# First FFN of a decoder step: gate and up by Strassen's scheme, and the down product as a stage of its own

## The chip, the cores and the metric

The kernel runs on one core of a Trainium2 chip. The metric is the device time of one launch in microseconds. Three runs of the kernel before took 2860.6, 2861.0 and 2862.41 us; the median, 2861.0, is the time before.

## What is computed

One layer of a hybrid decoder in f32 over 1088 tokens: 1024 of a prompt and 64 of a sample group. D_MODEL is 1024 and D_FF 2816 (22 blocks of 128 hidden columns). Cut to what matters here:

```
def swiglu(x, w_gu, w_down):
    gate, up = jnp.split(x @ w_gu, 2, axis=-1)
    return (jax.nn.silu(gate) * up) @ w_down

x = x + 0.5 * swiglu(rmsnorm(x, ffn1_norm), ffn1_w_gu, ffn1_w_down)   # the first FFN: what changes
h = rmsnorm(x, mix_norm); z = h @ w_in                                # 58 column blocks: attention, recurrence,
                                                                      # memory, gates
x = x + merged @ w_out
x = x + 0.5 * swiglu(rmsnorm(x, ffn2_norm), ffn2_w_gu, ffn2_w_down)   # the second FFN
```

## The kernel before

Features lie on the 128 partitions and tokens along the free dimension. The 1088 tokens are three chunks of 352, 368 and 368 columns (`CH`). Every f32 operand is split into two float32r parts, a high part (ScalarE copies it) and the remainder (VectorE subtracts), and every product is three matmuls: high by high, high by remainder, remainder by high (`mac3`, L179 to L181). Weights come as [128, 1024] units: SyncE's queue loads one (`load`, L141), ScalarE and VectorE split it (`split`, L153 and L154) into one of four buffers, and `ahead` keeps them ahead of use.

The first FFN (`ffn`) goes over 22 pairs: a pair is one gate and one up tile of 128 hidden columns. For each pair and chunk there are two products of 8 k-tiles by 3 matmuls. The norm's scale per token is applied after the product, from the row tile `rbc`, when the pair is evacuated (`evac`: VectorE from PSUM, Silu on ScalarE, the product of the two on GpSimd, then the split into `h`). So the first matmul needs x, its gains and a weight, but no norm. `DOWN` interleaves the down product: after each two or three pairs their rows of w_down are used at once, `h` stays in SBUF, and each down tile is added into x by VectorE (L348).

Each engine works through its own queue in order, and the order is that of the code: `tick`, called inside the products, runs side jobs one step at a time (`first`, `side`, `due`). SyncE's queue alone is ordered by the framework's scheduler. Along the first FFN go copies of the sample caches (`copies`, from DRAM to DRAM, about 1 MB each) and three calls of `bias_rows`, each a small DMA and two matmuls (L399) that TensorE waits for in its queue. After the last down group `part` splits x for the next layer.

Of the kernel before, what the change touches and what calls it, by code (L numbers as in the profile page):

```python
# [15 lines left out]
D = 1024  # L16
# [23 lines left out]
# rows of w_down taken together, and the width of their column blocks; the last rows stay whole  # L40
DOWN = [(0, 2, 512), (2, 2, 512)] + [(k, 3, 256) for k in range(4, 19, 3)] + [(19, 3, 1024)]
# [9 lines left out]
class Kernel:  # L51
    def __init__(self, ctx, tc, ins, cst, outs):
        self.ctx, self.tc, self.nc = ctx, tc, tc.nc
        self.i, self.c, self.o = ins, cst, dict(zip(_OUTS, outs))
        self.n = 0
        self.ticks = 0
        self.first, self.side, self.due, self.hurry = [], [], [], False
        self.raws, self.ready, self.using = [], [], 0
# [39 lines left out]
    def bank(self, tag, name=None):  # L98
        w = 1024 if tag == "s" else 512
        return self.ps.tile([128, w], F32, name=self.uid(name or tag), tag=tag, bufs=self.ps_bufs[tag])  # L100

# [1 line left out]
    def make_plan(self):  # L103
# [6 lines left out]
        def ffn(gu, dn):  # L110
            pair = lambda p: [col(gu, p), col(gu, KF + p)]
            plan, off = pair(0) + pair(1), 0
            for g, (k, nk, w) in enumerate(DOWN):
                if w == D:
                    return plan + [flat(dn, off + j * 128 * D, D) for j in range(nk)]
                k1, n1, _ = DOWN[g + 1]
                plan += pair(k1) + [flat(dn, off + j * 128 * nk * w, nk * w) for j in range(D // w)]
                plan += [u for p in range(k1 + 1, k1 + n1) for u in pair(p)]
                off += 128 * nk * D

# [12 lines left out]
        self.plan = ffn("w_gu1", "w_dn1") + mix + merge + outp + ffn("w_gu2", "w_dn2")  # L133
# [10 lines left out]
    def split(self, cuts=1):  # L144
        nc = self.nc
        if not self.raws:
            self.load()
        if self.raws:
            name, raw, n = self.raws.pop(0)
            spl = self.wspl.tile([128, 2, 1024], F32R, name=self.uid("ws"), tag="wspl")  # L150
            for j in range(cuts):
                e = slice(j * n // cuts, (j + 1) * n // cuts)
                nc.scalar.activation(spl[:, 0, e], raw[:, e], AF.Copy)  # L153
                nc.vector.tensor_tensor(out=spl[:, 1, e], in0=raw[:, e], in1=spl[:, 0, e].bitcast(F32), op=OP.subtract)  # L154
            self.ready.append((name, spl))
        while len(self.raws) < 2 and self.plan:
            self.load()

    def ahead(self):
        if len(self.ready) + self.using < 4:  # L160
            self.split()

    def unit(self, name, w):
        """The next unit: (j, c) -> both parts of the 128 columns from c of its k-tile j, w columns wide."""
        if not self.ready:
            self.split()
        got, spl = self.ready.pop(0)
        assert got == name, (got, name)
        self.using += 1
        return lambda j, c, n=128: tuple(spl[:, s, j * w + c:j * w + c + n] for s in range(2))  # L170

    def done(self):
        self.using -= 1

    def mac3(self, out, wx):
        nc = self.nc
        n = len(wx)
        for i, ((wh, wl), (xh, xl)) in enumerate(wx):
            nc.tensor.matmul(out, wh, xh, start=i == 0, stop=False)  # L179
            nc.tensor.matmul(out, wh, xl, start=False, stop=False)  # L180
            nc.tensor.matmul(out, wl, xh, start=False, stop=i == n - 1)  # L181
# [19 lines left out]
    # ---- rstd of tokens from the feature-major sums of their squares: token-major first, then as rows on every  # L201
    # partition ----
# [28 lines left out]
    def sumsq(self, k, src, acc, n, eng=None, tag="td"):  # L231
        """Add the squares of one feature tile into acc."""
# [11 lines left out]
    def setup(self):  # L244
# [4 lines left out]
        self.wraw = pool("wraw", 3)  # L249
        self.wspl = pool("wspl", 4)  # L250
        self.xgp = pool("xgp", 3)
# [18 lines left out]
        self.xs_d = [self.dram([128, KD, n], f"xs_d{c}") for c, (_, n) in enumerate(CH)]  # L270
        self.gate_d = self.dram([24, 128, NT], "gate_d")
# [6 lines left out]
    def load_x(self):  # L278
        """The first chunk and weight in small pieces, one after the other."""
        nc = self.nc  # L280
        part = lambda c, k, n: nc.sync.dma_start(self.x[:, k:k + n, CH[c][0]:sum(CH[c])],
                                                 self.i["x"][k:k + n, :, CH[c][0]:sum(CH[c])].rearrange("k p n -> p k n"))
        part(0, 0, 2)
        self.load(2)
        for k in (2, 4, 6):
            part(0, k, 2)
        self.load()
        for c in (1, 2):
            for k in (0, 4):
                part(c, k, 4)  # L290
        nc.sync.dma_start(self.ident, self.c["ident"])

    def start_x(self, c):
        t0, n = CH[c]
        self.new_xg(c)
        for k in range(KD):
            if c == 0 and k == 2:
                self.split(2)
            self.split_x(c, k, self.x[:, k, t0:t0 + n], self.v["ffn1_norm"])
        if c == 0:  # L300
            self.split()

# [1 line left out]
    def ffn(self, gu, dn, order, begin, after, fill):  # L304
# [38 lines left out]
        def down_tile(ks, part, o, c):  # L343
            t0, n = CH[c]
            ps = self.mm_bank("pd")
            self.mac3(ps[:, :n], [(part(j), tuple(h[k][:, s, t0:t0 + n] for s in range(2))) for j, k in enumerate(ks)])
            xa = self.x[:, o, t0:t0 + n]
            nc.vector.tensor_tensor(out=xa, in0=xa, in1=ps[:, :n], op=OP.add)  # L348
            self.tick()

        gate_up(0)
        gate_up(1)
        for g, (k, nk, w) in enumerate(DOWN[:-1]):
            k1, n1, _ = DOWN[g + 1]
            gate_up(k1)
            for o0 in range(0, KD, w // 128):
                wd = self.unit(dn, w)
                for o in range(o0, o0 + w // 128):
                    for c in range(3):
                        down_tile(range(k, k + nk), lambda j: wd(j, (o - o0) * 128), o, c)  # L360
# [3 lines left out]
        k, nk, w = DOWN[-1]  # L364
        wd = [self.unit(dn, w) for _ in range(nk)]
        for c in range(3):
            for o in range(KD):
                down_tile(range(k, k + nk), lambda j: wd[j](0, o * 128), o, c)
# [37 lines left out]
    def toeplitz(self, dst, g, h, col, rows, n):  # L406
        """dst[r, j] = bias row [g, h] at col - r + j."""
# [30 lines left out]
    def heads(self, g, hp):  # L438
        """q, k and v of one pair of heads; the rest of their work is queued."""
# [40 lines left out]
    def att_job(self):  # L480
        """Prompt attention, three blocks at a time at different stages."""
# [66 lines left out]
    def att_combine(self, pool):  # L548
        """Mix the three head groups of the prompt tokens, 128 at a time."""
# [24 lines left out]
    def mix_groups(self, o, A, H):  # L574
        """o [128, 3, A, H*64 + H + H]: values, -max, sum per head of group g; the mix replaces the values of group 0."""
# [35 lines left out]
    def sample_take(self, g, hp, z):  # L611
        """Keep the sample columns of one pair of heads: token-major, and queries apart by head."""
# [38 lines left out]
    def sample_piece(self, src, g, b, u):  # L651
        """[128, n, 256]: rows dil*i + 4u + c of batch b of a cache of group g."""
# [6 lines left out]
    def sample_scores(self, g):  # L659
        """Scores of one group over the caches, [cache row, batch, head, token]."""  # L660
# [126 lines left out]
    def mem_prep(self, mp):  # L787
        """The memory tokens, scaled by the norm's gains and split, and their rstd."""
# [55 lines left out]
    def mem_head(self, h, pool):  # L844
        """One memory head's queries; returns its attention over the prompt as a job."""
# [699 lines left out]
```

## Time and profile before

| | |
|---|---|
| median of three runs | 2861.0 us |
| span of the profiled execution | 2854.3 us |
| what lies around the span, by the median | 6.7 us |
| TensorE matmul, busy | 2801.9 us, 98% of the span, 16762 matmuls |
| VectorE, ScalarE, GpSimd busy | 1309.6, 748.5, 449.0 us |
| HBM read and written | 268.0 and 84.2 MB |

The profile has one execution with the span from its first to its last instruction; no time of that execution from outside is given, so the 6.7 us are the median less the span. A matmul's recorded duration overlaps the next one, so the pace of TensorE is read from the distance between starts (the step), not from the duration. "Idle before" is the engine's idle time just ahead of an instruction, with what ended it.

### The profile page before, as it was taken

How to read it: one execution, taken by the hardware profiler on the slowest of the kernel's cores; microseconds unless marked ns; L12 is line 12 of the kernel's file. 1: busy time of each engine (PE TensorE's matmuls, PEld its weight loads, DVE VectorE, ACT ScalarE, POOL GpSimd, SP SyncE). 2: the span in 40 equal slices, each digit the busy share in tenths (PEclk: the TensorE clock that was granted, in tenths of full speed). 3: DMA queues.
4: the chain of work that ended last, by engine and by line, in shares of the span. 5: the costliest groups of instructions: out<-in, count | busy, mean ns of one | idle time of the engine just before them, and what ended most of it. 6: DMA issues, size and time to landing. Idle time of an engine off the chain costs nothing. (4 is left out here: it accounts for less than half of the span.)

```text
span 2854.3 us, 40939 instructions
## 1 busy us (share of the span) xinstructions
PE 2801.9 (98%) x16762; PEld 2685.4 (94%) x16762; DVE 1309.6 (46%) x2204; ACT 748.5 (26%) x1306; POOL 449.0 (16%) x504
## 2 busy tenths in 40 slices
PE   8999999999999999999989999899999999999998
PEld 7999999999999879999978888899999999999998
DVE  6433333333364433666685445664444333333244
ACT  4112111111253212233334334333321111111112
POOL 3001000000030000112143111332210000000104
PEclk9999999999999999999999999999999999999999
DMA  4222221221243342665544321765222122122121
GB/s 155 78 96 72 84 76 62 84 77 62 77 167 120 97 128 71 186 194 183 169 154 147 120 79 56 255 189 191 89 74 74 67 78 78 67 78 78 67 74 63
DMA packets 142107, 308.03 MB, mean 108 GB/s; under 512 B 17800, under 2 KB 95816, under 8 KB 141248
## 3 DMA queue, kind: packets, MB, share of 16 engines
q1 hardware_dynamic: 141920, 305.42, 32.6%
q8 instruction: 132, 2.16, 0.3%
q14 instruction: 55, 0.45, 0.0%
HBM read 267.97 MB, written 84.19 MB: 123 GB/s over the span
## 5 line engine op out<-in xcount | busy, mean ns | idle before, releaser
L179 PE MATMUL pg<-xg,ws 128*128 128x368 f32 (+1 forms) x2112 | 696.4, 330 | 6.1 <-ACT ws L153 6.1
L181 PE MATMUL pg<-xg,ws 128*128 128x368 f32 (+1 forms) x2112 | 694.4, 329 | 2.0 <-DVE ws L154 2.0
L180 PE MATMUL pg<-xg,ws 128*128 128x368 f32 (+1 forms) x2112 | 690.2, 327 | 0.5 <-DVE xg L199 0.5
L179 PE MATMUL z<-xg,ws 128*128 128x368 f32 (+1 forms) x1392 | 479.4, 344 | 6.0 <-DVE ta L1092 6.0
L181 PE MATMUL z<-xg,ws 128*128 128x368 f32 (+1 forms) x1392 | 457.0, 328 | 0.0
L180 PE MATMUL z<-xg,ws 128*128 128x368 f32 (+1 forms) x1392 | 456.1, 328 | 0.0
L154 DVE TENSOR_TENSOR ws<-wr,ws 128x1024 fp32r<-128x1024 f32 (+2 forms) x257 | 306.8, 1195 | 235.4 <-ACT ws L153 235.2
L179 PEld LDWEIGHTS pg<-xg,ws 128*128 128x128 f32 x2112 | 398.8, 189 | 6.4 <-ACT ws L153 6.1
L181 PEld LDWEIGHTS pg<-xg,ws 128*128 128x128 f32 x2112 | 398.9, 189 | 2.7 <-DVE ws L154 2.7
L180 PEld LDWEIGHTS pg<-xg,ws 128*128 128x128 f32 x2112 | 398.7, 189 | 2.4 <-DVE xg L199 2.4
L153 ACT ACTIVATE ws<-wr 128x1024 fp32r<-128x1024 f32 (+2 forms) x257 | 253.6, 989 | 543.6 <-PE pd L181 373.7
L180 PE MATMUL pd<-h,ws 128*128 128x368 f32 (+1 forms) x1056 | 346.2, 328 | 0.0
L179 PE MATMUL pd<-h,ws 128*128 128x368 f32 (+1 forms) x1056 | 346.0, 328 | 0.0
L181 PE MATMUL pd<-h,ws 128*128 128x368 f32 (+1 forms) x1056 | 345.5, 327 | 0.0
L321 POOL TENSOR_TENSOR td<-sl,tb 128x352 f32<-128x352 f32 (+1 forms) x132 | 128.4, 973 | 1336.7 <-DVE tb L320 1302.9
L179 PEld LDWEIGHTS z<-xg,ws 128*128 128x128 f32 x1392 | 263.2, 189 | 28.2 <-issue 19.0
L348 DVE TENSOR_TENSOR x<-x,pd 128x368 f32<-128x368 f32 (+1 forms) x384 | 199.0, 530 | 189.6 <-PE pd L181 189.5
L180 PEld LDWEIGHTS z<-xg,ws 128*128 128x128 f32 x1392 | 263.4, 189 | 2.8 <-issue 0.3
L181 PEld LDWEIGHTS z<-xg,ws 128*128 128x128 f32 x1392 | 262.8, 189 | 0.0
L320 DVE SCALAR_TENSOR_TENSOR tb<-pg,rbc 128x352 f32<-128x352 f32 (+1 forms) x132 | 70.7, 535 | 316.9 <-PE pg L181 316.9
L179 PEld LDWEIGHTS pd<-h,ws 128*128 128x128 f32 x1056 | 198.3, 188 | 0.0
L181 PEld LDWEIGHTS pd<-h,ws 128*128 128x128 f32 x1056 | 198.3, 188 | 0.0
(267 smaller groups left out, 3145.0 us busy)
## 6 DMA issues: line engine op xcount, KB each, us to landing
wr<-in_w_gu_dram SPq DMA_DIRECT2D x87, 512.0 KB
wr<-in_w_in_dram SPq DMA_DIRECT2D x58, 512.0 KB
qb<-qs_d SPq DMA_DIRECT2D x48, 512.0 KB
out_sk_dram<-in_cache_k_dram SPq DMA_DIRECT2D x16, 1020.0 KB
out_sv_dram<-in_cache_v_dram SPq DMA_DIRECT2D x16, 1020.0 KB
wr<-in_w_dn_dram SPq DMA_DIRECT2D x40, 384.0 KB
kv<-in_cache_k_dram SPq DMA_DIRECT2D x24, 512.0 KB
kv<-in_cache_v_dram SPq DMA_DIRECT2D x24, 512.0 KB
```

The source lines that it names most:

```text
L153: nc.scalar.activation(spl[:, 0, e], raw[:, e], AF.Copy)
L154: nc.vector.tensor_tensor(out=spl[:, 1, e], in0=raw[:, e], in1=spl[:, 0, e].bitcast(F32), op=OP.subtract)
L179: nc.tensor.matmul(out, wh, xh, start=i == 0, stop=False)
L180: nc.tensor.matmul(out, wh, xl, start=False, stop=False)
L181: nc.tensor.matmul(out, wl, xh, start=False, stop=i == n - 1)
L320: nc.vector.scalar_tensor_tensor(tb, pu[:, :n], 0.5, self.rbc[:, t0:t0 + n], op0=OP.mult, op1=OP.mult)
L321: nc.gpsimd.tensor_tensor(out=td, in0=sl, in1=tb, op=OP.mult)
L348: nc.vector.tensor_tensor(out=xa, in0=xa, in1=ps[:, :n], op=OP.add)
```

## The change

The tokens are two halves of 544, each a pair of chunks of 272. For a pair of tiles (gate, up), for the k-tiles 0 to 3 and 4 to 7 and for the two chunks of a half, the product is a 2 by 2 block product. It is now done with seven products of 4 k-tiles on sums of blocks (Winograd's form) in place of eight. The sums of weight blocks are made per pair (`combined`: seven operands of 512 columns, each split by ScalarE and VectorE; two sums on VectorE, two on GpSimd). The sums of x blocks are made once per half (`operands`), from x that has been scaled by gain and norm beforehand (`square_half`, `scale`). So the norm of a half comes ahead of its first matmul. Products come in the order m1, m6, m7, m5, m2, m4, m3 (`OPS`). m2, m4 and m3 accumulate into the banks of m1, m7 and m5 after ScalarE or VectorE has read these (`swiglu`).

A call of `quad` is one pair's seven products for one half or both. `QUADS` runs pairs 0 to 3 for the first half alone, during which the second half's operands are made; then pairs 4 to 21 for both; then pairs 0 to 3 for the second half. The result of each goes to DRAM (`h_d`). The down product follows as its own stage (`down`) in 11 groups of two blocks; `hidden` reads a block back and splits it. x itself is loaded again when the last four quads begin. Weights are split in halves of 512 columns into seven buffers, and raw weights have four buffers, in the whole kernel. The second FFN keeps its scheme.

```diff
-        self.wraw = pool("wraw", 3)
-        self.wspl = pool("wspl", 4)
+        self.wraw = pool("wraw", 4)
+        self.wspl = pool("wspl", RING)
...
+TC, TH = 272, 544
+OPS = (1, 6, 7, 5, 2, 4, 3)
+ALONE = 4
+QUADS = ([(p, (0,)) for p in range(ALONE)] + [(p, (0, 1)) for p in range(ALONE, KF)] + [(p, (1,)) for p in range(ALONE)])
+RING = 7
...
+    def combined(self, name, g, u):
+        a11, a12, a21, a22 = g[:, :512], g[:, 512:], u[:, :512], u[:, 512:]
...
+        put(1, a11)
+        yield
+        put(4, a22)
+        tt(nc.vector, a22, a21, a22, OP.add)
+        tt(nc.vector, s2, a22, a11, OP.subtract)
+        tt(nc.gpsimd, a21, a11, a21, OP.subtract)
+        yield
+        put(6, s2)
+        yield
+        put(7, a21)
...
+        put(2, a12)
+        tt(nc.gpsimd, a12, a12, s2, OP.subtract)
+        yield
+        put(3, a12)
...
+    def operands(self, tp, xs, g, pool, eng):
...
+        def put(m, src):
+            t = (pool[1] if m in (4, 3) else pool[0]).tile([128, 2, 4, TC], F32R, name=f"xo{tp}{m}{self.uid('_')}", bufs=1)
+            nc.scalar.activation(t[:, 0], src, AF.Copy)
+            nc.vector.tensor_tensor(out=t[:, 1], in0=src, in1=t[:, 0].bitcast(F32), op=OP.subtract)
...
+        def less(out, x, y):
+            eng.tensor_tensor(out=out, in0=x, in1=y, op=OP.subtract)
...
+    def swiglu(self, p, tp, pool):
...
+            if m == 7:
+                new("uu", [2, TC], 3)
+                plus(t["uu"][:, 1], ps, t["mu"])
...
+                nc.gpsimd.tensor_tensor(out=sl, in0=sl, in1=t["uu"], op=OP.mult)
+                nc.sync.dma_start(self.h_d[p, :, tp * TH:(tp + 1) * TH], sl.rearrange("p j n -> p (j n)"))
...
+    def hidden(self, k, pool):
+        raw = pool.tile([128, NT], F32, name=self.uid("hr"), tag="hr", bufs=2)
+        nc.sync.dma_start(raw, self.h_d[k])
+        yield
+        h = pool.tile([128, 2, NT], F32R, name=self.uid("h"), tag="h", bufs=4)
+        nc.scalar.activation(h[:, 0, :], raw, AF.Copy, scale=0.5)
+        nc.vector.scalar_tensor_tensor(h[:, 1, :], raw, 0.5, h[:, 0, :].bitcast(F32), op0=OP.mult, op1=OP.subtract)
...
+    def second():
+        yield from K.square_half(1, xs[1], ev)
+        yield from K.operands(1, xs[1], K.v["ffn1_norm"], (xo1, xo1b), nc.gpsimd)
+    K.first.append(second())
+    K.hurry = True
+    for n, (p, tps) in enumerate(QUADS):
...
+        if n == KF:
...
+            for c, (t0, w) in enumerate(CH):
+                nc.sync.dma_start(K.x[:, :, t0:t0 + w], K.i["x"][:, :, t0:t0 + w].rearrange("k p n -> p k n"))
+            for k, nk, _ in DOWN1[:2]:
+                K.first += [K.hidden(k + j, pool) for j in range(nk)]
+        K.quad("w_gu1", p, tps, ev)
```

Where this moves instructions is shown at two places. The first is VectorE's queue at the start of the program. Before, `xg` is the x operand of a chunk, `ws` a split weight; the rows up to the first two weights are:

```order
L199 SCALAR_TENSOR_TENSOR xg_116<-x_101,vec,xg_116 128x352 x2
L154 TENSOR_TENSOR ws_121<-wr_103,ws_121 128x512 x2
L199 SCALAR_TENSOR_TENSOR xg_116<-x_101,vec,xg_116 128x352 x6
L154 TENSOR_TENSOR ws_140<-wr_109,ws_140 128x1024
L199 SCALAR_TENSOR_TENSOR xg_168<-x_101,vec,xg_168 128x368 x8
```

Two k-tiles of x and half a weight are enough for the first matmul there. Now, at the same place on VectorE (`xs` is a half of x, `xo` an x operand, `rbc` the norm as rows), from the norm's rows to the operand of m6, the second product:

```order
L318 COPY rbc<-t_164 128x272
L179 TENSOR_TENSOR ws_170<-wr_111,ws_170 128x512
L383 SCALAR_TENSOR_TENSOR xs_105<-xs_105,vec,rbc 128x544 x4
L389 TENSOR_TENSOR xo_21_181<-xs_105,xo_21_181 128x1088
L393 TENSOR_TENSOR xs_105<-xs_105 128x4x272
L383 SCALAR_TENSOR_TENSOR xs_105<-xs_105,vec,rbc 128x544 x2
L179 TENSOR_TENSOR ws_187<-wr_113,ws_187 128x512
L194 TENSOR_TENSOR wr_113<-wr_113 128x512
L194 TENSOR_TENSOR s_169<-wr_113,wr_111 128x512
L383 SCALAR_TENSOR_TENSOR xs_105<-xs_105,vec,rbc 128x544 x2
L393 TENSOR_TENSOR xs_105<-xs_105 128x4x272
L389 TENSOR_TENSOR xo_23_196<-xs_105,xo_23_196 128x1088
```

The work that came after the products (the norm) now stands ahead of them, and scalings, block sums and seven operands of 1088 columns stand in front of what the later products wait for. The second place is SyncE's queue where the last four quads begin. Before, around the first FFN's last pairs, there are weights and a cache copy alone:

```order
L141 DMA wr_5843<-in_w_gu_dram 128x1024
L141 DMA wr_5914<-in_w_gu_dram 128x1024
L141 DMA wr_5985<-in_w_dn_dram 128x1024
L1259 DMA out_sk_dram<-in_cache_k_dram 16x16320
L141 DMA wr_6061<-in_w_dn_dram 128x1024
```

Now, with `sl` the results of the quad before, `x` the reload and `hr` a hidden block read back:

```order
L488 DMA h_d<-sl_5044 128x544
L488 DMA h_d<-sl_5058 128x544
L1486 DMA out_sk_dram<-in_cache_k_dram 16x16320
L1552 DMA x_5131<-in_x_dram 128x8x352
L1552 DMA x_5131<-in_x_dram 128x8x368 x2
L495 DMA hr_5151<-h_d 128x1088
L165 DMA wr_5172<-in_w_gu_dram 128x1024
```

The first hidden block stands behind the whole of x. VectorE's queue in the first of these quads is, from the add of m6 (`mu`) to the adds of m7 and m5 (`uu`):

```order
L465 TENSOR_TENSOR mu_5153<-pg_5155,mu_5153 128x272
L179 TENSOR_TENSOR ws_5190<-wr_4945,ws_5190 128x512
L194 TENSOR_TENSOR wr_4945<-wr_4945 128x512
L194 TENSOR_TENSOR s_5168<-wr_4945,wr_4943 128x512
L499 SCALAR_TENSOR_TENSOR h_5196<-hr_5151,h_5196 128x1088
L465 TENSOR_TENSOR uu_5199<-pg_5177,mu_5153 128x272
L179 TENSOR_TENSOR ws_5214<-s_5168,ws_5214 128x512
L465 TENSOR_TENSOR uu_5199<-pg_5201,uu_5199 128x272
```

The remainder of that hidden block stands ahead of the add of m7, and m4 accumulates into m7's bank.

## Rows read from the trace of the kernel before

**Rows 1.** The page: TensorE's busy time, and the chain by engine.
```profile
PE 2801.9 (98%) x16762; PEld 2685.4 (94%) x16762; DVE 1309.6 (46%) x2204; ACT 748.5 (26%) x1306; POOL 449.0 (16%) x504
...
PE 46%; DVE 1%; ACT 0%; DMA 0%; POOL 0%; issue 0%; SPq 0%; DVEq 0%; POOLq 0%; ACTq 0%
```
**Rows 2.** Stretches: length, busy time of the engines (instructions), granted clock, DMA share, GB/s.
```profile
0.00:100.00 100.00, 88.67 (x506) 85.49 (x507) 59.04 (x97) 41.34 (x72) 29.10 (x31) 0.98 0.37 127
100.00:816.00 716.00, 712.43 (x4306) 709.24 (x4306) 273.38 (x458) 142.48 (x225) 85.29 (x106) 1.00 0.24 80
816.00:2854.00 2038.00, 2000.84 (x11954) 1890.63 (x11952) 977.17 (x1651) 564.72 (x1010) 334.65 (x368) 0.99 0.36 117
```
**Rows 3.** Timeline of TensorE (start, duration): the first matmul, and the first FFN's end.
```profile
6.08 0.66 PE L179 MATMUL pg<-xg,ws 128*128 128x352 f32 x1 [6.08 <-ACT ws L153]
...
815.91 0.32 PE L179 MATMUL z<-xg,ws 128*128 128x352 f32 x1
```
**Rows 4.** Timeline of TensorE: products' first matmuls, 24 apart; then two, 30 apart.
```profile
414.10 0.33 PE L179 MATMUL pg<-xg,ws 128*128 128x352 f32 x1
...
417.98 0.33 PE L179 MATMUL pg<-xg,ws 128*128 128x368 f32 x1
...
421.98 0.33 PE L179 MATMUL pg<-xg,ws 128*128 128x368 f32 x1
...
853.15 0.28 PE L179 MATMUL mk<-mg,ws 128*128 128x256 f32 x1
...
856.71 0.28 PE L179 MATMUL mk<-mg,ws 128*128 128x256 f32 x1
```
**Rows 5.** TensorE's groups by shape up to 816 us; each has two more lines alike.
```profile
L179 PE MATMUL pg<-xg,ws 128*128 128x368 f32 x704 | 233.4, 332 | 0.0
...
L179 PE MATMUL pd<-h,ws 128*128 128x368 f32 x352 | 116.8, 332 | 0.0
L179 PE MATMUL pg<-xg,ws 128*128 128x352 f32 x352 | 116.4, 331 | 6.1 <-ACT ws L153 6.1
...
L179 PE MATMUL pd<-h,ws 128*128 128x352 f32 x176 | 56.6, 322 | 0.0
```
**Rows 6.** DMA in the first 24 us, in 40 slices of 0.6 us.
```profile
GB/s 0 0 8 113 113 334 408 385 325 295 364 359 380 399 432 406 380 407 390 366 353 356 363 393 397 395 400 405 407 410 423 416 430 416 408 254 35 0 0 0
```
**Rows 7.** VectorE's groups by shape up to 816 us: busy, mean ns.
```profile
L154 DVE TENSOR_TENSOR ws<-wr,ws 128x1024 fp32r<-128x1024 f32 x51 | 63.1, 1239 | 43.9 <-ACT ws L153 43.9
L348 DVE TENSOR_TENSOR x<-x,pd 128x352 f32<-128x352 f32 x64 | 33.0, 517 | 19.7 <-PE pd L181 19.7
...
L154 DVE TENSOR_TENSOR ws<-wr,ws 128x768 fp32r<-128x768 f32 x20 | 19.2, 959 | 22.4 <-ACT ws L153 22.4
```
**Rows 8.** ScalarE's split of a weight, whole program.
```profile
L153 ACT ACTIVATE ws<-wr 128x1024 fp32r<-128x1024 f32 x183 | 192.4, 1052 | 481.9 <-PE pd L181 373.7 <-PE pg L181 54.3 <-PE z L181 34.4
```
**Rows 9.** GpSimd's groups by shape, whole program.
```profile
L690 POOL TENSOR_TENSOR qb<-qb,kv 128x1024 f32<-128x1024 f32 x24 | 57.6, 2398 | 235.1 <-DMA qb<-qs_d 151.9 <-DVE s L510 23.8 <-DVE st L538 16.6
L216 POOL TENSOR_TENSOR rs<-rs,mhalf 128x4 f32<-128x4 f32 x13 | 15.1, 1162 | 59.7 <-DVE rs L215 32.1 <-DVE rs L213 17.5 <-DVE rs L207 10.0
```
**Rows 10.** Timelines: VectorE with GpSimd busy beside it, GpSimd there, VectorE alone.
```profile
9.10 6.65 DVE L199 SCALAR_TENSOR_TENSOR xg<-x,vec,xg 128x352 fp32r<-128x352 f32 x6
...
11.06 1.10 POOL L1291 TENSOR_TENSOR acc<-acc,td 128x352 f32<-128x352 f32 x1
...
20.82 7.44 DVE L199 SCALAR_TENSOR_TENSOR xg<-x,vec,xg 128x368 fp32r<-128x368 f32 x13
```
**Rows 11.** Timeline of TensorE at a call of `bias_rows`.
```profile
150.72 1.13 PE L399 MATMUL t<-oh 32*4 32x512 f32 x4 [3.56 <-DMA oh<-in_rel_bias_dram]
...
152.50 0.49 PE L179 MATMUL pg<-xg,ws 128*128 128x352 f32 x1
152.79 0.49 PE L180 MATMUL pg<-xg,ws 128*128 128x352 f32 x1
```
**Rows 12.** The first FFN's last 26 us as a stretch, columns as in rows 2.
```profile
790.00:816.00 26.00, 26.00 (x163) 25.93 (x162) 22.41 (x41) 16.52 (x34) 18.91 (x17) 1.00 0.32 116
```

More of the change, by code (lines that the diff above doesn't have):

```diff
@@ L142, in load, with raw @@
             self.raws.append((name, raw, n))
-    def split(self, cuts=1):
-        nc = self.nc
+    def raw(self):
         if not self.raws:
             self.load()
[L148 to L157, printed above, removed]
@@ L159, in ahead, with part @@
-    def ahead(self):
-        if len(self.ready) + self.using < 4:
-            self.split()
-    def unit(self, name, w):
[L165 to L170, printed above, removed]
+        return self.raws.pop(0)
+    def part(self, src):
+        nc = self.nc
+        n = src.shape[1]
+        spl = self.wspl.tile([128, 2, 512], F32R, name=self.uid("ws"), tag="wspl")
+        nc.scalar.activation(spl[:, 0, :n], src, AF.Copy)
+        nc.vector.tensor_tensor(out=spl[:, 1, :n], in0=src, in1=spl[:, 0, :n].bitcast(F32), op=OP.subtract)
+        return spl
@@ new lines, in make @@
+    def make(self):
+        for _ in self.rest:
+            return
+        if self.raws or self.plan:
+            name, raw, n = self.raw()
+            if name in self.strassen:
+                self.rest = self.combined(name, raw, self.raw()[1])
+            else:
+                self.rest = self.halves(name, raw, n)
+            next(self.rest)
+            while len(self.raws) < 2 and self.plan:
+                self.load()
+    def ahead(self):
+        for _ in range(2):
+            if len(self.ready) + self.using < RING:
+                self.make()
@@ L293, in start_x @@
-    def start_x(self, c):
-        t0, n = CH[c]
[L295 to L301, printed above, removed]
+        rb = self.rbc[:, tp * TH:(tp + 1) * TH]
+        block = lambda i, j: xs[:, 4 * i:4 * i + 4, j * TC:(j + 1) * TC]
+        b11, b12, b21, b22 = (block(i, j) for i in range(2) for j in range(2))
+        got = self.xo[tp] = {}
@@ new lines, in operands, with square_half @@
+        less(b21, b21, b22)
+        yield
+        put(4, b21)
+        yield
+    def square_half(self, tp, xs, pool):
+        nc = self.nc
+        acc = None
+        for k in range(KD):
+            t = pool.tile([128, TH], F32, name=self.uid("sq"), tag="sl" if k else "uu", bufs=3)
+            nc.scalar.activation(t, xs[:, k, :], AF.Square)
+            if k:
+                nc.vector.tensor_tensor(out=acc, in0=acc, in1=t, op=OP.add)
+            else:
+                acc = t
+            if k % 2:
+                yield
+        r = [self.rstd(TC, acc[:, j * TC:(j + 1) * TC]) for j in range(2)]
+        yield
+        for j in range(2):
+            self.rows(self.rbc[:, tp * TH + j * TC:tp * TH + (j + 1) * TC], r[j], TC)
+        yield
@@ new lines, in quad @@
+    def quad(self, gu, p, tps, pool):
+        banks, steps = {}, {tp: self.swiglu(p, tp, pool) for tp in tps}
+        for m in OPS:
+            w = self.operand(gu, m)
+            for tp in tps:
+                bank = {2: 1, 4: 7, 3: 5}.get(m, m)
+                if bank == m:
+                    banks[tp, m] = self.mm_bank("pg")
+                ps, xo = banks[tp, bank][:, :TC], self.xo[tp][m]
+                part = lambda t, k: tuple(t[:, s, k] for s in range(2))
+                self.mac3(ps, [(tuple(w[:, s, k * 128:(k + 1) * 128] for s in range(2)), (xo[:, 0, k, :], xo[:, 1, k, :]))
+                               for k in range(4)], start=bank == m)
+                steps[tp](m, ps)
+            self.using -= 1
```

303 lines of the change are left out of this document (215 added, 88 removed).

## The prediction

> **What bounds the kernel now.** I read the page first. TensorE's matmuls are busy 98% of the span and nearly the whole chain that ended last is TensorE's [rows 1]; so the time is the number of matmuls by their step, and whatever holds TensorE up. Then the stretches: from 100 to 816 us TensorE is busy 712.4 of 716 us at the full clock while VectorE has 273; only the first 100 us leave a visible hole, 88.7 of 100 [rows 2]. The first FFN starts its matmuls at 6.1 us and gives way to the next layer's `z` at 815.9 us [rows 3]; that second number is what the change moves. Everything after it (2038 us [rows 2]) keeps its products.
>
> Next the step between starts. 24 matmuls of 352 columns take 3.88 us (0.1617 each), 24 of 368 take 4.00 (0.1667), 30 of 256 take 3.56 (0.1187) [rows 4]. Between 256 and 352 a column costs 0.000448 us, so one of 272 columns gets 0.1187 + 16 x 0.000448 = 0.1259 us. There is no sign yet of a floor set by weight loads, since 256 columns still run at 0.1187 with a load per matmul.
>
> **Columns saved.** Gate and up have 3 x 704 matmuls of 368 and 3 x 352 of 352 columns [rows 5]: 2112 x 0.1667 + 1056 x 0.1617 = 522.8 us. Now there are 22 pairs x 2 halves x 7 products x 12 matmuls = 3696 of 272 columns: 465.3 us. That removes 57.5 us of TensorE time. The down product keeps its 1056 + 528 matmuls [rows 5], 261.4 us. All of this lies on the path.
>
> **The start.** Before, TensorE begins at 6.1 us, because the norm is applied after the products. Now half of x (2.2 MB) must land, be squared, summed, turned into rows and multiplied in. DMA moves about 0.4 MB per us from 3 us on [rows 6], so the last piece is in at about 10; two squares, the last sum, two pow on GpSimd at about 1.1 us one after the other [rows 9], transposes and two copies give `rbc` at about 16.
>
> From there VectorE's queue sets the pace, not TensorE. I count it up to the add that the third quad's m4 waits for, and price it by the line through 1024 columns at 1.24 and 768 at 0.96 us [rows 7], 1.09 ns a column: 23 weight remainders of 512 columns at 0.68 = 15.6; 16 scalings of 544 at 0.71 = 11.4; 14 operand remainders and 4 block sums of 1088 at 1.31 = 23.6; 7 sums of squares at 0.71 = 5.0; 8 weight sums at 0.68 = 5.4; 12 adds of 272 columns from PSUM at 0.43 (352 take 0.52) = 5.2; the norm of the second half 1.5. Sum 67.7 us. After that add TensorE has two products and the fourth quad left, 108 matmuls, 13.6 us. So the fourth quad ends at 16 + 67.7 + 13.6 = 97 us at best.
>
> Three things come on top. VectorE idles where its queue has nothing but the remainder of what ScalarE is just copying: three times about 1.1 us (1024 columns take ScalarE 1.05 [rows 8]), 2.4 us for the first m3 weight (it waits for GpSimd's sum and then ScalarE), and about 2 us each at two of the second half's operands, whose block sums are GpSimd's, 1088 columns at 2.5 us (1024 take 2.40 [rows 9]): 9.5 us, from 5 to 14. Then the two engines slow each other: beside GpSimd six scalings took 6.65 us, 1.11 each; thirteen, nearly all with GpSimd idle, took 7.44, 0.57 each [rows 10]. GpSimd's 12 sums and products here are 6 x 1.2 + 2 x 1.3 + 4 x 2.5 = 20 us, three quarters of it beside VectorE work with two operands in SBUF, which loses half its pace: 7.2 us, bounds 0 and 15 (VectorE standing still). Last, TensorE waits so much that it starts after gaps at the lower of its two clocks: after a gap of 3.56 us its 352-column steps were 0.29 us [rows 11]: 1.5 us, as most of these steps are off VectorE's path. I take 97 + 9.5 + 7.2 + 1.5 = 115 us, bounds 93 (a little overlap between instructions, no idling) and 130.
>
> The Trainium skill (SBUF — State Buffer, Who interferes with whom) says that a VectorE instruction with two SBUF inputs and a GpSimd instruction that reads SBUF exclude each other: whichever starts first holds the shared ports to its end. The rows show a weaker thing, half the pace rather than none. By the rule the loss would be all of 15 us in place of 7.2; that case is in the third rival.
>
> **The middle.** 18 quads of both halves are 168 matmuls or 21.2 us each, and VectorE has about 11 us of work in each: 7 remainders, 2 sums, 10 adds. The seven split operands and five or more products between an add and the product that accumulates on it cover it, so I cost its stalls at nothing; if that cover fails, each product can lose up to 0.4 us. `bias_rows` stays: its three calls have about 1.3 us of matmuls and slow starts each and one had a wait of 3.56 us plus slow steps [rows 11]. The matmuls are queued two products behind their DMA; two products are now 3 us and not 8, so I take a wait of about 5: 10 us in all, bounds 4 and 18.
>
> **The last four quads.** All the matmuls but the first four quads', 3360, take 423.0 us. But when the 23rd quad begins, SyncE issues the stores of the quad before (after GpSimd's product, about 2.6 us in), a cache copy, the whole of x (4.46 MB), and only then the first hidden block (0.56 MB). With store and copy that is 6.3 MB at 0.4 MB per us [rows 6], landing about 19 us into the quad if transfers go in the order of issue. ScalarE waits for it in its queue and VectorE behind, ahead of the add of m7; m4 accumulates on that bank. Copy 1.1, remainder 1.3, add 0.4: m4 starts at 21.8 us, where five products of 1.51 us would let it at 7.5. That is 14.3 us and 1.2 for the slow clock: 15.5, bounds 0 (the block overtakes x) and 22 (a DMA rate a quarter lower).
>
> **Down and the rest.** x's second reading and the blocks read back lie beside 24 us of TensorE per group. The last group splits x as before, but a tile has 6 matmuls instead of 9, 1.0 us. Over the old last 26 us VectorE was 86% busy [rows 12] with tiles of 1.5 us, so at 1.0 it falls behind by about 6 us over 24 tiles; six banks hide about half: 3 us, bounds 0 and 7. Norm sums at the end 2. For the smaller weight halves after 816 us I take 1, bounds -3 and 6.
>
> **The sum.** 115 + 423.0 + 10 + 15.5 + 261.4 + 3 + 2 = 829.9 us for the first `z`, against 815.9: 14 us later. With 1 for the rest the span is 2854.3 + 15 = 2869.3. The median of the runs is 6.7 us over the span of the profiled execution (2861.0), so 2876. The saving of 57.5 us goes to the start and the one wait.
>
> **Rivals.** First, faster: VectorE's queue runs almost without idling or port loss (98 us at the fourth quad), the hidden block lands early (3), `bias_rows` costs 6: 98 + 423 + 6 + 3 + 261.4 + 2 = 793.4, 22.5 less, 2839 us. For it speaks that of the start only the 97 us are counted and the 18 on top are inferred; against it that those 97 are fixed by count already, and that x stands in front of the hidden block in the queue. It decides where fourth quad and wait together stay under 108 us. Second, no change that can be told: 105 at the fourth quad, a wait of 10, bias 8, last group 1: 810.4, 5.5 less, with the rest's 1 about 2857, up to 2866 with slightly larger terms. Third, slower still: GpSimd's instructions shut VectorE out for their whole length (8 us more at the start), and in the last four quads, where VectorE has 8 us of work, 1.3 for a hidden block and the same loss of ports against 10.5 us of TensorE, the adds run late by 2 us each: 16 more, 2892. That the arithmetic does not shrink (a 272-column step as long as a 352-column one, 0.16) would cost another 126 us; the 256-column rows exclude it, and it gets no chance of its own.
>
> **How the numbers follow.** Forecast 0.45 (2867 to 2885), third rival 0.20, no change 0.17, faster 0.18. About 0.2%, 5.7 us, is what a measurement of this kernel can tell from none. So faster 0.18, same 0.17, slower 0.65. The range is 2843 to 2894: it takes in the second rival, the upper part of the first and most of the third, and leaves out about 0.1 at each end.
>
> **What would show it.** gate/up steps near 0.126 us; VectorE nearly always busy from 16 to 100 us while TensorE is under half; the fourth quad's last product near 115; 21.2 us a quad after it; one wait of about 14 us early in the 23rd quad that ends with a hidden block's remainder; the first `z` near 830. I am wrong if the fourth quad ends before 100 us, or if that wait is missing; and if middle quads take more than 22 us the loss is larger than I say.

## The result, and the profile after

The changed kernel takes 2938.95 us (median of four runs, 2934.54 to 2942.79) against 2861.7 us before: a ratio of 1.0272, 95% interval 1.0257 to 1.0286, so 77 us slower. The forecast was 2876 us, range 2843 to 2894: the side was right, the size was not. The profiled execution is the longest of the four (2942.79 us), its span is 2941.0 us.

The page after, two lines that answer to [rows 1]:

```profile
PE 2779.3 (95%) x17299; PEld 2658.4 (90%) x17299; DVE 1525.5 (52%) x2725; ACT 843.2 (29%) x1657; POOL 517.6 (18%) x524
...
PE 83%; DMA 6%; DVE 5%; issue 2%; ACT 2%; POOL 1%; SPq 1%; DVEq 0%; ACTq 0%; POOLq 0%
```

TensorE's busy time fell, but it now has holes, and the chain that ended last has DMA in it, which had no share before. The stretches, with the columns of [rows 2]; 885 us is where the first `z` now stands:

```profile
0.00:100.00 100.00, 45.79 (x252) 42.59 (x252) 72.23 (x100) 38.19 (x58) 25.52 (x19) 0.90 0.28 97
100.00:885.00 785.00, 718.23 (x5095) 710.95 (x5096) 453.82 (x792) 219.02 (x406) 159.13 (x138) 0.95 0.35 122
885.00:2941.00 2056.00, 2015.29 (x11954) 1904.82 (x11952) 999.49 (x1835) 585.98 (x1194) 332.91 (x368) 0.99 0.36 115
```

The first 100 us have 46 us of TensorE where they had 89, the stretch to `z` has 67 us of holes where it had 4, and the unchanged products behind it take 18 us longer. Four rows of TensorE's timeline (start, duration) give the ends and the step, answering to [rows 3, 4]:

```profile
21.91 0.59 PE L273 MATMUL pg<-xo,ws 128*128 128x272 f32 x1 [5.06 <-ACT xo L388]
...
413.84 0.29 PE L273 MATMUL pg<-xo,ws 128*128 128x272 f32 x1
...
424.36 0.29 PE L273 MATMUL pg<-xo,ws 128*128 128x272 f32 x1
...
884.94 0.32 PE L273 MATMUL z<-xg,ws 128*128 128x352 f32 x1
```

84 matmuls of one half quad lie between the two middle rows: 10.52 us, 0.1253 each. The arithmetic shrinks as counted.

The same trace gives the rest of the account. Each half quad's distance to the next, less 10.525 us, is what it lost; the fourth quad ended at 126.05 us (0.16 us behind the next start, as recorded durations overlap).

| term up to the first `z` | forecast, us | measured, us |
|---|---|---|
| fourth quad ends | 115 | 126.0 |
| 3360 matmuls of gate and up | 423.0 | 421.0 |
| three `bias_rows` | 10 | 34.0 (1.3, 31.5, 1.3) |
| waits for weights in the middle | 0 | 11.9 (five, 0.5 to 5.7) |
| 23rd quad, first half | 15.5 | 19.7 |
| the three half quads behind it | 0 | 4.0 |
| down stage to `z` | 266.4 | 268.6 |
| first `z` | 829.9 | 884.9 |
| rest, against before | +1 | +17.7 |

The largest single wait has its own row, and so has the one of the 23rd quad, with what ended them:

```profile
221.25 2.07 PE L626 MATMUL t<-oh 32*4 32x512 f32 x4 [27.78 <-DMA oh<-in_rel_bias_dram]
...
575.24 0.59 PE L273 MATMUL pg<-xo,ws 128*128 128x272 f32 x1 [16.93 <-DVE uu L465]
```

The second is the forecast one: VectorE's add of `uu` stands behind a hidden block's remainder, that behind ScalarE's copy, and that waited 17.9 us for the block. The five waits in the middle also end with an add of `uu`, but what is late there is a weight; the longest of them, with ScalarE's row ahead of it:

```profile
390.00 0.63 ACT L178 ACTIVATE ws<-wr 128x512 fp32r<-128x512 f32 x1 [9.88 <-DMA wr<-in_w_gu_dram]
...
394.53 0.60 PE L273 MATMUL pg<-xo,ws 128*128 128x272 f32 x1 [2.82 <-DVE uu L465]
```

The largest wait, at 221 us, had been put at about 5 us. Half of its cause shows in the DMA from 170 to 200 us, in 40 slices of 0.75 us (busy share in tenths, then GB/s):

```profile
DMA  8196037987030030030050030003001114789899
GB/s 337 41 337 198 6 52 202 500 339 289 16 172 0 0 172 0 0 172 0 0 194 0 0 172 0 0 0 172 0 0 55 49 55 183 276 194 202 195 255 335
```

Where nothing but a cache copy is left (178 to 192 us), 129 KB land every 2.4 us: two pieces of 64.5 KB at a time, 54 GB/s. That copy of 1.03 MB takes 20.3 us; eight such copies (lines 1469 to 1486, the middle cache group, 2 rows x 8 pieces) run between 172 and 389 us, 19.0 to 20.9 us each. Two of them stand in front of this wait, as SyncE's rows show:

```profile
172.98 0.26 SPq L628 DMA_DIRECT2D bias_d<-br  x1
...
193.36 2.49 SPq L630 DMA_DIRECT2D skew_d<-bias_d  x4
...
197.00 0.69 SPq L1486 DMA_DIRECT2D out_sk_dram<-in_cache_k_dram  x1
...
198.19 0.75 SPq L620 DMA_DIRECT2D oh<-in_rel_bias_dram  x1
```

The first copy (172.4 to 192.7 us) held up the store of the bias row before, so that SyncE could issue the next one's load only at 198 us; the second (201.2 to 220.2 us) held up that load, for which TensorE waited until 221 us.

The copies were as slow before. The kernel before from 120 to 160 us, in slices of 1 us, shows one, and [rows 11] show the wait behind it:

```profile
DMA  0000058968974002020110202001689922027897
GB/s 0 0 0 0 7 76 336 334 168 231 332 243 181 0 16 129 0 129 0 65 65 0 129 0 129 0 0 45 107 274 367 352 77 56 0 98 213 250 272 189
```

### The profile page after: what moved, and what is told of

Same layout as the page of the kernel before. It is cut to its first block, busy times and chain, and to the rows that moved or that the text cites. A ratio compares the mean times of both kernels' runs of the same rounds, so it can differ in the third digit from the quotient of the medians.

```text
span 2941.0 us, 43467 instructions
## 1 busy us (share of the span) xinstructions
PE 2779.3 (95%) x17299; PEld 2658.4 (90%) x17299; DVE 1525.5 (52%) x2725; ACT 843.2 (29%) x1657; POOL 517.6 (18%) x524
## 4 chain that ended last, share of the span: by engine, by line
PE 83%; DMA 6%; DVE 5%; issue 2%; ACT 2%; POOL 1%; SPq 1%; DVEq 0%; ACTq 0%; POOLq 0%
PE pg L273 10%; PE pg L274 10%; PE pg L275 10%; PE z L273 7%; PE z L274 7%; PE z L275 7%; PE pd L274 6%; PE pd L273 6%; PE pd L275 6%; DMA wr<-in_w_gu_dram 2%; PE po L275 2%; PE po L274 2%; PE po L273 2%; PE t L982 2%; PE o L763 1%
## 5 line engine op out<-in xcount | busy, mean ns | idle before, releaser
L179 DVE TENSOR_TENSOR ws<-wr,ws 128x512 fp32r<-128x512 f32 (+1 forms) x570 | 409.7, 744 | 233.0 <-ACT ws L178 232.3
L178 ACT ACTIVATE ws<-wr 128x512 fp32r<-128x512 f32 (+1 forms) x570 | 329.3, 603 | 689.5 <-PE pd L275 373.8
L273 PE MATMUL pg<-xo,ws 128*128 128x272 f32 x1232 | 366.4, 297 | 66.4 <-DVE uu L465 42.7
L274 PE MATMUL pg<-xo,ws 128*128 128x272 f32 x1232 | 362.9, 295 | 1.5 <-DVE xo L389 1.5
L275 PE MATMUL pg<-xo,ws 128*128 128x272 f32 x1232 | 361.5, 293 | 0.6 <-DVE ws L179 0.6
L273 PE MATMUL pg<-xg,ws 128*128 128x368 f32 (+1 forms) x1056 | 346.4, 328 | 0.0
L274 PE MATMUL pg<-xg,ws 128*128 128x368 f32 (+1 forms) x1056 | 346.3, 328 | 0.0
L275 PE MATMUL pg<-xg,ws 128*128 128x368 f32 (+1 forms) x1056 | 346.2, 328 | 0.0
L534 DVE TENSOR_TENSOR x<-x,pd 128x368 f32<-128x368 f32 (+1 forms) x456 | 235.9, 529 | 181.9 <-PE pd L275 181.9
L273 PEld LDWEIGHTS pg<-xo,ws 128*128 128x128 f32 x1232 | 239.6, 195 | 71.1 <-DVE uu L465 45.4
L274 PEld LDWEIGHTS pg<-xo,ws 128*128 128x128 f32 x1232 | 239.9, 195 | 2.1 <-DVE xo L389 2.1
L275 PEld LDWEIGHTS pg<-xo,ws 128*128 128x128 f32 x1232 | 239.8, 195 | 0.9 <-DVE ws L179 0.9
L275 PEld LDWEIGHTS pd<-h,ws 128*128 128x128 f32 x1056 | 198.9, 188 | 0.0
```

What stands on the lines that cost most here:

```text
L178: nc.scalar.activation(spl[:, 0, :n], src, AF.Copy)
L179: nc.vector.tensor_tensor(out=spl[:, 1, :n], in0=src, in1=spl[:, 0, :n].bitcast(F32), op=OP.subtract)
L273: nc.tensor.matmul(out, wh, xh, start=start and i == 0, stop=False, **more)
L274: nc.tensor.matmul(out, wh, xl, start=False, stop=False, **more)
L275: nc.tensor.matmul(out, wl, xh, start=False, stop=i == n - 1, **more)
```

## The experiments

All times are medians of four runs or more; the kernel before, run on the same chips, had medians of 2858.8 to 2860.7 us.

### What the cache copies cost

The first edit gives each slow copy to two copies of one row in 16 pieces; the second does the same in the kernel before.

```diff
-                nb, cut = ((8, 1), (2, 1), (1, 2))[g]
+                nb, cut = ((8, 1), (1, 1), (1, 2))[g]
...
+                        if g == 1 and b % 2:
+                            pieces[-1].append(piece)
```

> The eight middle cache copies (2 rows x 8 pieces of 64.5 KB) go as two copies each of one row in 16 pieces of 32 KB; the bytes and places of issue are the same. Theory A: in the changed kernel each of these copies takes 20 us at 54 GB/s, only two transfers at a time, and everything behind it on SyncE's queue waits: the 28 us of TensorE in front of the second bias product and the five waits of 0.4 to 3.0 us for weights between 300 and 395 us. Then the new form should take 3 to 6 us a copy, and the time falls by about 40, to 2895-2905 us. Theory B: the bias rows and weights are late for another reason (their place behind two halves' work, or their own size), and the form of the copies does nothing: 2934-2943 us.

> The kernel before with the same other form of the eight copies. Theory A: its weights are asked for some 48 us ahead, so slow copies hold up almost nothing there; only the 3.7 us wait for a bias row at 147 us goes: 2855-2859 us. Theory B: nothing changes: 2860-2863 us.

Measured: 2905.92 us, 33 less. A pair of split copies takes 3.6 to 5.4 us, the five waits for weights are gone, and the three `bias_rows` cost 13.0 us in place of 34.0: 21.0 + 11.9 = 32.9 us, the whole gain (theory A had 1 to 11 us more). The longest wait that is left there:

```profile
200.05 2.07 PE L626 MATMUL t<-oh 32*4 32x512 f32 x4 [6.04 <-DMA oh<-in_rel_bias_dram]
```

In the kernel before it gave 2852.01 us, ratio 0.997 (0.996 to 0.9981): 3 us under theory A's range, and the only kernel here that does all the work and is faster than the one before. Its profiled execution, the longest of eight, has the first `z` 4.2 us earlier, about the one wait; where the rest of the 8.7 us comes from is not shown.

Is it the queue that they stand in, or their form? The next run leaves the form and moves them to ScalarE's queue; the one after leaves the queue and the pieces and swaps two dimensions.

```diff
-            self.tc.keep_in_program_order(self.nc.sync.dma_start(d, s))
+            self.tc.keep_in_program_order((self.nc.scalar if s.shape[0] == 2 else self.nc.sync).dma_start(d, s))
```

> The same eight slow cache copies in their old form (2 rows x 8 pieces of 64.5 KB), but issued by ScalarE on its own DMA queue. Theory A (a queue hands its transfers over in order, and what hurts is to stand behind a 20 us copy): the copies still take about 20 us, but the 28 us wait for the bias row shrinks to 6 or less and the waits for weights go: 2898-2910 us, like the split copies (2906). Theory B (a copy in this form slows the other transfers themselves, whatever queue it is in): less than half of the 33 us is won, 2923-2940 us.

```diff
-                        pieces.append(tuple(y.rearrange("b (q e) -> b q e", q=16 // nb)
+                        pieces.append(tuple(y.rearrange("b (q e) -> q b e" if g == 1 else "b (q e) -> b q e", q=16 // nb)
```

> The eight slow cache copies keep their 16 pieces of 64.5 KB and SyncE's queue; only the order of the two outer dimensions is swapped, 8 pieces x 2 rows and not 2 rows x 8 pieces. Theory A (the pieces are dealt to the DMA engines by the outermost dimension: 2 makes two engines carry all, as the traces show two packets of 64.5 KB at a time, and whatever has a share on these two engines waits, in any queue): eight run at a time, a copy takes about 5 us, and the time is 2898-2910 us, as with the split copies. Theory B (the size of the pieces or the rows they come from make them slow): 20 us a copy and 2934-2943 us as the changed kernel.

On ScalarE's queue the time rose to 2951.94 us, over both theories' ranges. The copies took 20.4 to 21.2 us as before, and the transfers on SyncE's queue, which no longer stood behind them, were late all the same. ScalarE's waits from 160 to 400 us (total, times, longest) and VectorE's longest from 190 to 230 us:

```profile
ACT sl L480 <- DMA h_d<-sl: 80.9, 7, 18.0
```

```profile
DVE br L627 <- DMA br<-c_offs_dram: 23.1, 1, 23.1
```

ScalarE now waits up to 18.0 us for a store of a hidden half, which holds the tile that it wants next. The packets say why: between 178 and 190 us of that run every 2.46 us land two of 64.5 KB and two of 2176 B, the store's. The store's other packets were through by then; these go one by one between the copy's pieces. That these are the packets on the two DMA engines that carry the copy is read from this pattern; no row names a packet's DMA engine. With the dimensions swapped the time was 2906.85 us, and a copy took 5.9 to 6.9 us with eight pieces at a time. The DMA of that run from 170 to 200 us:

```profile
DMA  1818900195543547479972000000002709901097
GB/s 22 345 61 302 714 9 0 16 748 208 202 202 133 218 202 309 169 172 265 325 284 66 0 0 0 0 0 0 0 0 83 279 20 366 694 12 37 6 695 288
```

So theory A of the first run came within 1 us of its range and fell in its reason: not the place in a queue, but two of sixteen engines given away for 20 us. The Trainium skill (DMA: Bandwidth & Descriptors, Why a DMA increments its semaphore by 16 and not by 1) states that a transfer goes to as many engines as divide the slowest dimension that is not 1, at most 16; the runs agree: outermost dimensions of 2, 8 and 16 gave two, eight and sixteen pieces at a time. The Trainium skill (DMA: Bandwidth & Descriptors, Queues, rings and completion order) says that an engine takes turns between queues packet by packet; the pattern of 64.5 KB and 2176 B packets agrees.

### The 23rd quad

```diff
-            for c, (t0, w) in enumerate(CH):
-                nc.sync.dma_start(K.x[:, :, t0:t0 + w], K.i["x"][:, :, t0:t0 + w].rearrange("k p n -> p k n"))
             for k, nk, _ in DOWN1[:2]:
                 K.first += [K.hidden(k + j, pool) for j in range(nk)]
+        if n > KF and n <= KF + 3:
+            t0, w = CH[n - KF - 1]
+            nc.sync.dma_start(K.x[:, :, t0:t0 + w], K.i["x"][:, :, t0:t0 + w].rearrange("k p n -> p k n"))
```

> The second reading of x (4.46 MB) is issued in three pieces at the 24th, 25th and 26th quad and no longer ahead of the first hidden blocks at the 23rd. Theory A (the hidden block waits behind x in SyncE's queue): the 17.1 us wait in the 23rd quad goes but for 1 to 3 us: 2920-2926 us. Theory B (the hidden block is late because it is written and read back through DRAM, or ScalarE and VectorE are late themselves): at least 8 us of the wait stay: 2931 us or more.

Measured: 2930.31 us, 8.6 less. The half quad lost 8.5 us in place of 19.7, and the wait was

```profile
562.92 0.59 PE L273 MATMUL pg<-xo,ws 128*128 128x272 f32 x1 [5.81 <-DVE uu L465]
```

so x in front of the block is two thirds of it: ScalarE's first hidden copy starts at 560.1 us and not at 572.4. What is left lies behind store, cache copy and block, which no run took apart. And 4.8 us came back in the last half quad, because the fourth block now stood behind pieces of x (7.2 us of waiting on ScalarE at 597.9 us). The expected gain of 13 to 19 us was too much; the mechanism holds.

### The start

First what GpSimd's sums do to VectorE: all of them go to VectorE.

```diff
-        tt(nc.gpsimd, a21, a11, a21, OP.subtract)
+        tt(nc.vector, a21, a11, a21, OP.subtract)
...
-        yield from K.operands(1, xs[1], K.v["ffn1_norm"], (xo1, xo1b), nc.gpsimd)
+        yield from K.operands(1, xs[1], K.v["ffn1_norm"], (xo1, xo1b), nc.vector)
```

> All of GpSimd's block sums (the second half's four of 1088 columns and two weight sums of 512 per pair) move to VectorE. Theory A: at the start GpSimd costs VectorE its pace (29 weight remainders took 0.97 us each and 16 scalings 0.97, where they take 0.68 and 0.71 alone, 12 us together) and is waited for (9 us of ScalarE); VectorE gets 4 x 1.29 + 8 x 0.69 = 10.7 us more work in the first four quads, so the fourth quad ends 5 to 10 us earlier than 126 and the time is 2929-2936 us. Theory B: VectorE's queue alone sets the pace there, and the 10.7 us come on top: fourth quad at 134 or later, 2945-2952 us.

Measured: 2931.61 us, 7.3 less; the fourth quad ends at 119.9 us. VectorE from 16 us to that point, by shape (busy, mean ns, idle before): first the changed kernel, then this one.

```profile
L179 DVE TENSOR_TENSOR ws<-wr,ws 128x512 fp32r<-128x512 f32 x29 | 27.8, 968 | 6.2 <-ACT ws L178 6.2
L389 DVE TENSOR_TENSOR xo<-xs,xo 128x1088 fp32r<-128x1088 f32 x14 | 18.8, 1362 | 7.7 <-ACT xo L388 7.7
L383 DVE SCALAR_TENSOR_TENSOR xs<-xs,vec,rbc 128x544 f32<-128x544 f32 x16 | 14.8, 967 | 0.0
```

```profile
L179 DVE TENSOR_TENSOR ws<-wr,ws 128x512 fp32r<-128x512 f32 x29 | 21.6, 759 | 4.0 <-ACT ws L178 4.0
L389 DVE TENSOR_TENSOR xo<-xs,xo 128x1088 fp32r<-128x1088 f32 x14 | 17.8, 1286 | 5.3 <-ACT xo L388 5.3
L383 DVE SCALAR_TENSOR_TENSOR xs<-xs,vec,rbc 128x544 f32<-128x544 f32 x16 | 11.7, 778 | 0.0
```

The same instructions run 10 us shorter in sum and wait 4.6 us less, which pays for some 10.7 us of sums taken over and more. Single rows of the changed kernel show how GpSimd costs VectorE its pace:

```profile
76.39 2.47 POOL L393 TENSOR_TENSOR xs<-xs 128x1088 f32<-128x1088 f32 x1 [4.49 <-DVE xo L389]
76.58 2.83 DVE L179 TENSOR_TENSOR ws<-wr,ws 128x512 fp32r<-128x512 f32 x1
...
103.74 2.48 POOL L393 TENSOR_TENSOR xs<-xs 128x1088 f32<-128x1088 f32 x1 [3.70 <-DVE xo L389]
103.87 2.89 DVE L179 TENSOR_TENSOR ws<-wr,ws 128x512 fp32r<-128x512 f32 x1
```

A remainder of 0.68 us that starts just behind GpSimd's sum ends 0.55 us after it: VectorE stands still until GpSimd is through. The third such pair, at 85.74 us, does the same. So do the six scalings of [rows 10] when taken one by one: each ends 0.38 to 0.39 us after one of GpSimd's instructions, which take 1.05 to 1.27 us there.

Then two runs that leave work out of the start: the first FFN's norm with its sums of squares, and, on top of the three mends (the split copies, x read later, the sums on VectorE), the norm and all operands of x but one.

```diff
-                nc.vector.scalar_tensor_tensor(xs[:, k, :], xs[:, k, :], self.vec[:, g + k:g + k + 1], rb,
-                                               op0=OP.mult, op1=OP.mult)
+                pass
...
         nc = self.nc
+        yield
+        return
...
         def put(m, src):
+            if m != 1:
+                got[m] = got[1]
+                return
```

> The first FFN's norm is left out (the sums of squares, rstd and the scaling of x ahead of the operands); all other work stays. Theory A (the start is the length of VectorE's queue behind the norm): VectorE loses 16 scalings of 0.97 us, 14 sums of 0.72-0.87 us, two waits for rbc (8 us) and starts when x lands, at about 8 us and not at 17: the fourth quad ends at 85 to 95 us and not at 126, the time is 2898-2908 us. Theory B (weights, GpSimd's sums and ScalarE set the start): the fourth quad ends at 105 or later, 2918 us or more.

> With the split copies, x later and the weights' block sums on VectorE; left out are the first FFN's norm and, of the operands of x, all block sums and all but the first of seven remainders and copies (one operand stands for all seven). Theory A (the arithmetic saves its 57 us, and what eats it is making the operands ahead of the first quads): the fourth quad ends at 65 to 80 us and not at 120, the time is 2836-2852 us, under the kernel before. Theory B (making the weights' operands holds the quads anyway): fourth quad at 95 or later, 2865 us or more.

Without the norm: 2908.38 us, fourth quad at 95.1 us, 31 earlier; the upper end of what theory A had. With the operands left out as well: 2836.83 us, ratio to the kernel before 0.9924 (0.9909 to 0.9939), fourth quad at 63.0 us. The three mends alone have 2893.05 us (below) and 119.9, so what is left out here is worth 56 to 57 us. Its stretch from 16 us to there and its first `z`:

```profile
16.00:63.00 47.00, 43.82 (x331) 42.62 (x330) 41.84 (x71) 24.18 (x45) 4.11 (x3) 1.00 0.48 165
```

```profile
782.59 0.32 PE L273 MATMUL z<-xg,ws 128*128 128x352 f32 x1
```

The same columns for the changed kernel, where TensorE has 61 of 110 us:

```profile
16.00:126.00 110.00, 60.80 (x358) 57.81 (x359) 88.87 (x114) 43.05 (x67) 31.96 (x18) 0.84 0.20 68
```

So Strassen's saving is there, as long as the operands cost nothing: the first `z` comes 33 us before the kernel before, and 29 us before that kernel with the same split copies (811.7 us), against which the time is 15 us less.

Last, two pairs in place of four for one half alone (`ALONE = 2`).

> Two pairs and not four are done for the first half of the tokens alone. Theory A (VectorE's queue sets the start: the second half's operands, 14.8 + 9 us and more, cost the same, but two pairs' weights, about 9 us of VectorE, need not be made twice): the start loses 75 to 79 us of TensorE and not 84, 2928-2936 us. Theory B (the alone quads are what covers the second half's operands; with two fewer TensorE just waits longer): 2939-2952 us.

Measured: 2960.35 us, 21 more. The start did what theory A says: the first four half quads end at 118.4 us, 7.6 earlier. But TensorE's waits from 120 to 640 us (total, times, longest) show where more was lost:

```profile
PE t L626 <- DMA oh<-in_rel_bias_dram: 50.2, 2, 27.6
PE pg L273 <- DVE uu L465: 19.9, 2, 17.3
PE pd L273 <- DVE x L534: 4.9, 1, 4.9
```

Now two of the three `bias_rows` met a slow copy (143.8 to 164.1 and 220.3 to 240.1 us), 26.9 us more in all than in the changed kernel; and the time behind the first `z` is 7.7 us longer. Neither theory had that; the larger part is the copies' doing once more.

### Together, and what lies behind the first FFN

> The changed kernel with the three mends together: split copies (-33 us alone), x read later (-8.6), GpSimd's block sums on VectorE (-7.3). Theory A (three waits at different places): they add up, 2886-2894 us. Theory B (the waits share a cause, the length of SyncE's queue, so one mend takes the next one's gain): 2896-2905 us.

Measured: 2893.05 us: 46 less, where the single gains add up to 49. They lie at three places, and the kernel is still 1.2% over the one before (1.0118, 1.0102 to 1.0135), and 41 us over that one with its copies split.

> Split copies, x read later, block sums on VectorE and two pairs alone, together. Theory A (four places, they add up): the three mends gave 2893, with the gain of two pairs alone 2882-2890 us, still over the kernel before. Theory B (VectorE is too busy with all block sums for a shorter start): 2893 us or more.

Measured: 2903.57 us, 10 more than with four pairs alone. The start gained 7 us again, but two `bias_rows` waited (7.7 and 11.3 us) and a down tile 4.5 us, and the time from the first `z` to the last matmul was 2052 us in place of 2040. (The profiled execution, of which these are read, is the longest of its four, 6.6 us over their median.) Why that stretch grew is not shown.

The 17.7 us behind the first `z` were to be the weights' halves, tried in the kernel before (`RING = 7` halves of 512 columns; its first FFN as it was):

> The kernel before, with all its weights split in halves of 512 columns into a ring of 7 such halves (before: 4 whole units of 1024), as the change does it; its first FFN stays as it was. Theory A (the smaller, shorter ring is why all behind the first FFN takes 17 us longer in the changed kernel): the time behind the first z rises by 12 to 18 us, 2872-2880 us. Theory B (it is the other placement of tiles, or a late VectorE after the new down stage): the time behind the first z stays within 4 us, 2857-2866 us.

Measured: 2873.16 us, in theory A's range and for another reason. The first `z` came 14 us later, at 830.1 us, and from there to the last matmul it took 2029.0 us against 2028.7. One wait, 3.56 us in [rows 11], grew by 12.7 us, which is most of the loss; a slow copy runs just ahead of it, from 139.7 to 159.8 us:

```profile
163.22 2.07 PE L425 MATMUL t<-oh 32*4 32x512 f32 x4 [16.25 <-DMA oh<-in_rel_bias_dram]
```

So theory A fell: the halves alone do not lengthen the stretch. What the changed kernel's trace shows of the 17.7 us: the order of TensorE's 11953 instructions there is the same as before, and 5.4 us are lost from 22 to 27 us after `z`, where ScalarE waits for the memory tokens, which SyncE issued 7.5 us after `z` (before: 1.5):

```profile
899.93 0.51 ACT L1026 ACTIVATE mg<-mraw,vec 128x256 fp32r<-128x256 f32 x1 [7.92 <-DMA mraw<-in_mem_dram]
```

With the halves alone the tokens were issued late too, 6.5 us after `z`, and ScalarE waited 7.0 us; TensorE was 3.8 us behind there and had made it good before the end, so the halves may have a share in this wait. Some 3.5 us lie around the first branch products (`po`), 1.3 at the end; about 4 us are the second FFN's steps, 2112 of 368 columns taking 355.7 us in place of 352.3, the same in every run built on the changed kernel and not in the two built on the kernel before. The rest is spread in small pieces. The 17.7 us are not firm to the microsecond: the other runs built on the changed kernel have 11.8 to 25.4, and the kernel before with split copies 3.3. None of these was undone by a run; why the steps are longer stays open.

## Why the prediction was wrong

- **The sign, and the columns: right.** 0.1253 us a step against 0.1259; TensorE's saving of 57 us was lost at the start and in waits, as the sum had it.
- **The failed step is the middle**, "so I cost its stalls at nothing", with the wait of "about 5" for `bias_rows`. The stalls measured 11.9 us and the three `bias_rows` 34.0 where 10 were forecast. The cover named was VectorE's; what failed was DMA. Transfers were priced at 0.4 MB per us [rows 6], and the middle cache copies, which run at 0.054, were not priced at all. The trace of before held both signs: the 54 GB/s on the mean after a copy's issue, and the 3.56 us of [rows 11], which were read as the bias row's own. Before, a load had long slack; now a quad is 21 us and a slow copy 20, and one is issued in nearly every quad. The split copies take away 33 us, and with them `bias_rows` cost 13 us, within the bounds of 4 to 18.
- **The start: right in kind, 11 us short, within its bounds.** VectorE's queue sets it (31 us earlier without the norm). The weight remainders took 0.97 us and not 0.68 and the scalings 0.97 and not 0.71, 12 us together where 7.2 were taken for the shared ports. The step behind the 7.2 is "half the pace rather than none": taken one by one, the scalings of [rows 10], from which it was read, stand still until GpSimd is through, as the third rival had it. And VectorE idled 21 us of 110, 18 of them up to the add that the third quad's m4 waits for, where 9.5 were taken.
- **The 23rd quad: mechanism right**, 19.7 us against 15.5. (The bytes ahead of the block add up to 6.6 MB with it and not 6.3, which gives the same 19 us.) The third rival had the adds of the last four quads late by 2 us each; the three half quads behind that wait lost 4.0 us in all.
- **The rest: wrong**, 17.7 us against 1 (-3 to 6). It was costed by the smaller weight halves alone; these by themselves left the stretch as long as before, and the loads ordered late behind the new down stage were not looked at. Its cause stays open in the main.
- **The sum.** Slow copies 33, rest 17, start 11, 23rd quad and after 8, `bias_rows` without the slow copies 3, down 2, less 2 for the steps: 72 us over the forecast span of 2869.3, and the profiled span is 2941.0. The median is 63 over its forecast, as the profiled execution was the longest of its four and 6.7 us had been put around the span, where that execution has 1.8.

## What to carry to other kernels

A scheme that saves multiplications is paid for by the operands made ahead of the first one: price the queue of the engine that makes them up to the point where the main engine runs free, and at the pace it has beside its neighbours. When a change shortens the time between a load and its use, look through the trace for the slowest transfer of any kind that shares the DMA engines, not for the mean rate. And write a DRAM-to-DRAM copy with a large outermost dimension: 16 or 8 did here what 2 did not. An instruction that takes longer beside another engine is best read row by row, not by its mean.

## What was not expected of the hardware

- A copy of 1.03 MB took 19 to 21 us as 2 rows x 8 pieces, 6 to 7 us as 8 x 2 of the same pieces, and 3.6 to 5.4 us as two copies of 16 smaller pieces.
- Moving the slow copies to another engine's queue made the kernel slower (2952 us against 2939): ScalarE then waited up to 18 us for a store of 272 KB, some of whose packets went one by one between pieces of 64.5 KB.
- VectorE's remainders of 512 columns beside GpSimd's sums took 0.97 us on the mean, and 0.76 with these sums on VectorE itself. On the mean this looks like a slower pace; row by row it is the exclusion that the prediction's third rival took from the Trainium skill (SBUF — State Buffer, Who interferes with whom), and the trace agrees: 2.83 us for a remainder that takes 0.68 alone, ending 0.55 us behind GpSimd's sum.
